# The last down-projection of a two-layer decoder as seven half-size products

## The chip, the cores and the metric

The kernel runs on one core of a Trainium2 chip. The metric is the device time of one execution in microseconds (us), the median over the runs shown; lower is better. The engines are TensorE (PE; the loads of its stationary operand are listed as PEld), VectorE (DVE), ScalarE (ACT), GpSimd (POOL) and SyncE (SP). SP, ACT and POOL each issue transfers on a queue of their own.

## The reference

A trunk of two layers works on `x` of 512 tokens by 1024 features: a Mamba-2 mixer and a gated FFN with a short convolution, then differential attention and a second such FFN. Only the end matters here:

```
def conv_ffn(x, ln_g, up_w, conv_w, conv_b, down_w):
    u = causal_dwconv(rms_norm(x, ln_g) @ up_w, conv_w, conv_b)
    gate, up = u[..., :FFN_DIM], u[..., FFN_DIM:]        # FFN_DIM = 2816
    return (jax.nn.silu(gate) * up) @ down_w             # (512 x 2816) @ (2816 x 1024)
...
    x = x + ff.astype(x.dtype)                           # the output of the last layer
```

All data is float32.

## The kernel before

Every large product is computed in a reduced format three times over: each operand is split into a high part (a copy rounded to `float32r` by ScalarE) and a low part (the difference, by VectorE), and `mm3` adds high x high, high x low and low x high into one PSUM bank (lines 170 to 172 of the kernel). The residual stream is kept feature-major: `xT[m]` holds features 128 m to 128 m + 127 of all 512 tokens.

**Weights.** A list `plan` names all weight chunks in the order of use. `emit_chunk` takes the next one: SP loads 512 KB into a `raw` tile (three buffers), ACT writes the high part `wh` (line 143), DVE the low part `wl` (line 144), three buffers each. `chunk(key)` hands a chunk to the matmuls and emits further ones, so that two are prepared ahead. The matmuls of a chunk of the FFN are 24, each 128x128 by 128x512.

**The FFN** (`ffn`). The 22 blocks of 128 hidden features are done in two passes, 12 and then 10. For each block, `u_block` computes the gate and then the up product (8 feature blocks, 24 matmuls each), scales by the norm (DVE, line 758), applies the convolution (one ACT operation, line 759, two DVE operations, line 761), and the block ends with SiLU (ACT), the product gate x up (DVE, line 774), and the split into `hh` (ACT, line 775) and `hl` (DVE, line 776). Then the down-projection of the pass follows: for each of four groups of 256 output features, three chunks of the weight feed two PSUM banks, with the weights stationary and the hidden activations of 512 tokens moving. DVE adds each bank to `xT[m]` (line 454).

**The end** (`store`). In the last pass of the last FFN, DVE adds each bank to the stream in two halves (line 800), PE transposes the sum to token-major (line 802), ACT copies it out of PSUM (line 803) and SP and ACT issue the transfers to `out` (line 804): 32 transposes in all.

**Order.** The program is written with tiles; a scheduler places the instructions on the engines by readiness and by their place in the program, adds all waits, and each engine then works strictly in the order so fixed. There are eight PSUM banks, four of tag `mm` and four of tag `aux`.

Of the kernel before, what the change touches and what calls it, by code (L numbers as in the profile page):

```python
# [9 lines left out]
F32 = mybir.dt.float32  # L10
F32R = mybir.dt.float32r
# [28 lines left out]
def trunk_kernel(ctx: ExitStack, tc, x, ssm_ln_g, ssm_in_w, ssm_conv_w, ssm_conv_b, ssm_dt_bias,  # L40
# [23 lines left out]
    def w_cols(w, k0, nk, c0, ncol):  # L64
        return w[k0 * P:(k0 + nk) * P, c0:c0 + ncol].rearrange("(k p) c -> p k c", p=P), nk, ncol
# [20 lines left out]
            out_chunks(g - 1)  # L86
    out_chunks(NG - 1)

    def ffn_plan(l):
        for h, (p0, p1) in enumerate(((0, HALF), (HALF, NPAIR))):  # L90
            for p in range(p0, p1):
                plan.append(("g%d_%d" % (l, p), *w_cols(ffn_up_w[l], 0, KB, p * P, P)))
                plan.append(("u%d_%d" % (l, p), *w_cols(ffn_up_w[l], 0, KB, FFN + p * P, P)))
# [20 lines left out]
    ffn_plan(1)  # L114

    AHEAD = 2
    ready = []
# [4 lines left out]
    def emit_chunk(pin=lambda i: i):  # L122
        i = state["next"]
        if i >= len(plan):
            return
        state["next"] = i + 1
        key, src = plan[i][:2]
        nk, ncol = plan[i][2:4]
# [4 lines left out]
        sync.dma_start(raw[:, :n].rearrange("p (k c) -> p k c", k=nk), src)  # L133
        if len(plan[i]) > 4:

            for k in range(nk):
                ks = slice(k * ncol, (k + 1) * ncol)
                g = c2[:, plan[i][4] + k:plan[i][4] + k + 1]
                act.activation(wh[:, ks], raw[:, ks], AF.Copy, scale=g)
                dve.scalar_tensor_tensor(out=wl[:, ks], in0=raw[:, ks], scalar=g,  # L140
                                         in1=wh[:, ks].bitcast(F32), op0=ALU.mult, op1=ALU.subtract)
        else:
            pin(act.activation(wh[:, :n], raw[:, :n], AF.Copy))  # L143
            pin(dve.tensor_tensor(out=wl[:, :n], in0=raw[:, :n], in1=wh[:, :n].bitcast(F32), op=ALU.subtract))  # L144
        ready.append((key, wh[:, :n].rearrange("p (k c) -> p k c", k=nk),
                      wl[:, :n].rearrange("p (k c) -> p k c", k=nk)))
# [39 lines left out]
    g1 = cp.tile([P, KB], F32, name="g1")  # L186
    rs = cp.tile([P, NT], F32, name="rs")

    xTt = rp.tile([P, KB, T], F32, name="xT")
    xT = [xTt[:, k, :] for k in range(KB)]  # L190
# [21 lines left out]
    with tc.tile_pool(name="ph0", bufs=1) as p0:  # L212
# [53 lines left out]
                                         op0=ALU.mult, op1=ALU.subtract))  # L266

        def keep(h, q, on):
            o = xTt[:, 2 * q:2 * q + 2, half[h]]
# [469 lines left out]
        run(out_proj(NG - 1, *prev, norm))  # L739


    def ffn(l, norm, bp, gnext, nnext):
        with tc.tile_pool(name="ffn_h%d" % l, bufs=1) as hp, tc.tile_pool(name="ffn%d" % l, bufs=1) as fp:
            rr = []

            def u_block(j, p):
                key = "%s%d_%d" % ("gu"[j], l, p)
                wh, wl = chunk(key)
                ps = mm_bank("ps_" + key)
                for k in range(KB):  # L750
                    mm3(ps, wh[:, k, :], wl[:, k, :], xgh[k], xgl[k], k == 0, k == KB - 1)
                if not rr:
                    rr.append(norm.row())
                r = rr[0]
                col = lambda t: cf[l][:, 88 * j + 22 * t + p:88 * j + 22 * t + p + 1]
                u = fp.tile([P, T], F32, tag="u", name="u" + key, bufs=3)
                v = fp.tile([P, T], F32, tag="v%d" % j, name="v" + key, bufs=3)
                dve.tensor_tensor(out=u, in0=ps, in1=r, op=ALU.mult)  # L758
# [4 lines left out]
                return v  # L763

            for p0, p1 in ((0, HALF), (HALF, NPAIR)):
                last = p1 == NPAIR
                hh, hl = [], []
# [12 lines left out]
                for c in range(4):  # L780
                    pss = [mm_bank("ps_d%d_%d_%d" % (l, p0, 2 * c + i)) for i in range(2)]
                    for k0 in range(0, n, 4):
                        wh, wl = chunk("d%d_%d_%d" % (l, c, p0 + k0))
                        for i in range(2):
                            for k in range(k0, min(n, k0 + 4)):
                                mm3(pss[i], wh[:, k - k0, i * P:(i + 1) * P],
                                    wl[:, k - k0, i * P:(i + 1) * P], hh[k], hl[k], k == 0, k == n - 1)
                    for i in range(2):
                        m = 2 * c + i
                        if last and nnext is None:  # L790
                            store(m, pss[i], fp)
                        else:
                            add_to_stream(m, pss[i], gnext, nnext if last else None)

    def store(m, ps, fp):
        pt = aux_bank("ot%d" % m)
        o = fp.tile([P, NT, P], F32, tag="o", name="o%d" % m, bufs=3)
        for j in range(2):
            h = slice(j * 256, (j + 1) * 256)
            dve.tensor_tensor(out=xT[m][:, h], in0=ps[:, h], in1=xT[m][:, h], op=ALU.add)  # L800
            for b in (2 * j, 2 * j + 1):
                pe.transpose(pt[:, b * P:(b + 1) * P], xT[m][:, b * P:(b + 1) * P], ident)
            act.activation(o[:, 2 * j:2 * j + 2, :], pt[:, h].rearrange("p (a b) -> p a b", a=2), AF.Copy)
            (sync if j else act).dma_start(
                out[0, h, m * P:(m + 1) * P].rearrange("(b p) c -> p b c", p=P), o[:, 2 * j:2 * j + 2, :])

    norm_kv = Norm(bp, "kv")
    ffn(0, norm, bp, None, norm_kv)
# [252 lines left out]
```

## Time and profile before

| what | value |
|---|---|
| median of 3 runs | 1394.48 us (1394.02 to 1394.83) |
| span of the profiled execution, first to last instruction | 1396.8 us (no other time of this execution is given) |
| PE busy | 1373.6 us, 98% |
| DVE busy | 916.4 us, 66% |
| ACT busy | 668.1 us, 48% |
| POOL busy | 94.2 us, 7% |
| mean granted TensorE clock | 0.991 of full speed |
| last FFN, from its first matmul to the end | 1023.3 to 1396.8 us |
| read from and written to DRAM | 131.72 MB, 2.25 MB |

Busy times are sums of instruction durations on one engine; matmuls overlap, so the time between the starts of two matmuls says more than the length of one. A row of the timeline gives the start in us, the duration in us, engine, line, operation, output and inputs, shapes and count, and in brackets the idle time before it with what ended it. A row of a group gives the busy time in us, the mean in ns, and the idle time ahead of the group's instructions by what ended it. "Landing" of a transfer is the time from its issue to its completion.

### The profile page before, as it was taken

Reading aid. Unit: us, or ns where it says so; the run is one execution under the profiler, and the core shown is the slowest. Engines: PE = TensorE matmul, PEld = TensorE weight load, DVE = VectorE, ACT = ScalarE, POOL = GpSimd, SP = SyncE. Lnnn points to the kernel's source line nnn. Section 1 sums busy time; section 2 is a strip of 40 time slices with the busy share of each in tenths; the row PEclk is TensorE's granted clock in tenths of the full one; section 3 lists DMA queues with packets and bytes.
Section 4 is the critical chain, followed back from the end, with each engine's and each line's share of the span. In section 5 each row is a group of like instructions: output and inputs, shape, how many; then the busy total and the mean of one; then the engine's idle time right before and its main releaser. Section 6 shows DMA issues by size and latency. Waiting matters only on the chain.

```text
span 1396.8 us, 17046 instructions
## 1 busy us (share of the span) xinstructions
PE 1373.6 (98%) x6475; PEld 1111.0 (80%) x6475; DVE 916.4 (66%) x1537; ACT 668.1 (48%) x1104; POOL 94.2 (7%) x120
## 2 busy tenths in 40 slices
PE   8999999999999999999999999999999999999998
PEld 6878787787788888888888787786778888888886
DVE  4889878678767775257754546747677774367741
ACT  4588553733254443134433547857654443144431
POOL 4140300300030000000001000000020000000000
PEclk8999999999999999999999999999999999999999
DMA  5463433422233332333323322221133333333332
GB/s 152 119 182 103 144 91 105 130 79 81 79 102 91 92 105 91 105 92 95 101 83 98 117 91 76 61 77 52 46 91 105 91 99 97 92 104 91 98 92 68
DMA packets 187620, 135.09 MB, mean 97 GB/s; under 512 B 6541, under 2 KB 176977, under 8 KB 187537
## 3 DMA queue, kind: packets, MB, share of 16 engines
q1 hardware_dynamic: 180736, 120.84, 29.3%
q0 software_dynamic: 4496, 12.05, 2.8%
q10 hardware_dynamic: 2304, 1.10, 0.3%
q8 instruction: 51, 0.84, 0.2%
q14 instruction: 33, 0.26, 0.1%
HBM read 131.72 MB, written 2.25 MB: 96 GB/s over the span
## 4 chain that ended last, share of the span: by engine, by line
PE 83%; DVE 7%; ACT 6%; issue 2%; DMA 1%; POOL 1%; POOLq 0%; SPq 0%; ACTq 0%; DVEq 0%
PE ps_u L170 6%; PE ps_u L171 6%; PE ps_u L172 6%; PE ps_d L170 6%; PE ps_d L171 6%; PE ps_d L172 6%; PE ps_g L170 6%; PE ps_g L171 6%; PE ps_g L172 6%; PE ps_in L172 4%; PE ps_in L171 4%; PE ps_in L170 4%; PE ps_o L171 2%; PE ps_o L172 2%; PE ps_o L170 2%
## 5 line engine op out<-in xcount | busy, mean ns | idle before, releaser
L170 PE MATMUL ps_u<-xgh,wh_u 128*128 128x512 f32 x352 | 137.9, 392 | 0.0
L171 PE MATMUL ps_u<-xgl,wh_u 128*128 128x512 f32 x352 | 137.7, 391 | 0.0
L171 PE MATMUL ps_g<-xgl,wh_g 128*128 128x512 f32 x352 | 137.0, 389 | 0.5 <-DVE xgl L366 0.5
L170 PE MATMUL ps_d<-hh,wh_d 128*128 128x512 f32 x352 | 137.5, 391 | 0.0
L172 PE MATMUL ps_u<-xgh,wl_u 128*128 128x512 f32 x352 | 137.4, 390 | 0.0
L172 PE MATMUL ps_d<-hh,wl_d 128*128 128x512 f32 x352 | 137.3, 390 | 0.0
L170 PE MATMUL ps_g<-xgh,wh_g 128*128 128x512 f32 x352 | 137.0, 389 | 0.0
L171 PE MATMUL ps_d<-hl,wh_d 128*128 128x512 f32 x352 | 137.0, 389 | 0.0
L172 PE MATMUL ps_g<-xgh,wl_g 128*128 128x512 f32 x352 | 136.9, 389 | 0.0
L171 PE MATMUL ps_in<-xgl,wh_in 128*128 128x512 f32 x312 | 123.6, 396 | 0.0
L170 PE MATMUL ps_in<-xgh,wh_in 128*128 128x512 f32 x312 | 123.3, 395 | 0.0
L172 PE MATMUL ps_in<-xgh,wl_in 128*128 128x512 f32 x312 | 122.6, 394 | 0.0
L144 DVE TENSOR_TENSOR wl_d<-wr_d,wh_d 128x1024 fp32r<-128x1024 f32 (+1 forms) x48 | 54.5, 1135 | 91.8 <-ACT wh_d L143 91.6
L143 ACT ACTIVATE wh_d<-wr_d 128x1024 fp32r<-128x1024 f32 (+1 forms) x48 | 47.5, 990 | 129.4 <-PE ps_d L171 115.3
L775 ACT ACTIVATE hh<-vg 128x512 fp32r<-128x512 f32 x44 | 27.8, 631 | 114.9 <-DVE vg L774 114.9
L758 DVE TENSOR_TENSOR uu<-ps_u,nr_f 128x512 f32<-128x512 f32 x44 | 30.4, 692 | 79.4 <-PE ps_u L172 79.4
L172 PEld LDWEIGHTS ps_u<-xgh,wl_u 128*128 128x128 f32 x352 | 66.5, 189 | 13.9
L171 PEld LDWEIGHTS ps_g<-xgl,wh_g 128*128 128x128 f32 x352 | 66.0, 188 | 14.4 <-DVE xgl L366 0.8
L170 PEld LDWEIGHTS ps_u<-xgh,wh_u 128*128 128x128 f32 x352 | 66.5, 189 | 13.8
L171 PEld LDWEIGHTS ps_u<-xgl,wh_u 128*128 128x128 f32 x352 | 66.5, 189 | 13.6
L170 PEld LDWEIGHTS ps_g<-xgh,wh_g 128*128 128x128 f32 x352 | 66.1, 188 | 14.1 <-ACT xgh L365 0.5
L172 PEld LDWEIGHTS ps_g<-xgh,wl_g 128*128 128x128 f32 x352 | 66.1, 188 | 13.8
(334 smaller groups left out, 3002.8 us busy)
## 6 DMA issues: line engine op xcount, KB each, us to landing
wr_g<-in_ffn_up_w_dram SPq DMA_DIRECT2D x44, 512.0 KB, 3.9
wr_u<-in_ffn_up_w_dram SPq DMA_DIRECT2D x44, 512.0 KB, 3.8
wr_in<-in_ssm_in_w_dram SPq DMA_DIRECT2D x40, 512.0 KB, 3.9
wr_d<-in_ffn_down_w_dram SPq DMA_DIRECT2D x40, 512.0 KB, 3.5
m<-cumd POOLq DMA_DIRECT2D x16, 512.0 KB, 4.2
wr_out<-in_ssm_out_w_dram SPq DMA_DIRECT2D x16, 512.0 KB, 3.5
wr_k<-in_kv_w_dram SPq DMA_DIRECT2D x8, 512.0 KB, 3.8
wr_q<-in_q_w_dram SPq DMA_DIRECT2D x8, 512.0 KB, 4.0
```

The source lines that it names most:

```text
L143: pin(act.activation(wh[:, :n], raw[:, :n], AF.Copy))
L144: pin(dve.tensor_tensor(out=wl[:, :n], in0=raw[:, :n], in1=wh[:, :n].bitcast(F32), op=ALU.subtract))
L170: pe.matmul(ps, wh, xh, start=start, stop=False)
L171: pe.matmul(ps, wh, xl, start=False, stop=False)
L172: pe.matmul(ps, wl, xh, start=False, stop=stop)
L758: dve.tensor_tensor(out=u, in0=ps, in1=r, op=ALU.mult)
L775: act.activation(h, ga, AF.Copy)
```

## The change

The last FFN gets a function of its own, `last_ffn`. Its down-projection uses Strassen's method (the variant with seven products and shared sums): tokens are split in two halves of 256, the K dimension in even and odd blocks of 128, and the output features in two halves of 512. Each of the seven products is a product of half the size in all three dimensions.

- **Residual.** `turn` transposes the stream into token-major tiles `xt[b]` (128 tokens by 1024 features) with 32 transposes and eight ACT copies, after the first two pairs of hidden blocks. The space of the feature-major stream is then used again for weights.
- **Hidden activations.** `hidden(q)` does the blocks 2q and 2q + 1, and DVE forms the four sums `S1` to `S4` (each 128x256); one ACT and one DVE instruction split all seven left operands (1792 columns) into `hh` and `hl`.
- **Weights.** `fetch` loads the four quadrants of the weight of a pass in 1 MB transfers on SP's queue, two pairs into the pass. `weights` forms the right operand of products 5, 6, 7 and 4 by a subtraction in place on DVE, and splits it (ACT, DVE), up to 1024 columns per chunk. The quadrants are no longer loaded through `raw`.
- **Passes.** There are three: pairs 0 to 3, 4 to 7, 8 to 10. In each, the chunks come in the order of `STEPS`: products 1, 5, 2 for the first two pairs, then for the others, then 6, 7, 3, 4. Hidden activations (128 tokens) are stationary and weights (512 columns) moving.
- **Results.** Product 1 starts bank X, and 6 and 7 go on adding to it; 5 starts Y, and 3 goes on; 2 and 4 have banks of their own. After each product `add` copies the bank with ACT into a tile `ev` (tag `u`, three buffers, shared with `u_block`) and GpSimd issues a transfer that adds it to its quadrant of `xt` (product 7 goes to two quadrants). In the last pass that holds for products 1, 5 and 6; the results of 2, 7, 3 and 4 are added by DVE from PSUM to `xt`, and SP and ACT send finished quadrants to `out` directly.

The core of the diff:

```
-    rp = ctx.enter_context(tc.tile_pool(name="residual", bufs=1, side="right"))
+    rp = ctx.enter_context(tc.tile_pool(name="residual", bufs=2, side="right"))
...
+    PASSES = ((0, 4), (4, 8), (8, 11))
+    STEPS = ((1, 5, 2), (6,), (7,), (3,), (4,))
...
-                v = fp.tile([P, T], F32, tag="v%d" % j, name="v" + key, bufs=3)
+                v = fp.tile([P, T], F32, tag="v%d" % j, name="v" + key, bufs=nb)      # 2 in last_ffn
...
+            def turn(b, c):
+                ps = aux_bank("xt%d_%d" % (b, c))
+                for k in range(4):
+                    pe.transpose(ps[:, k * P:(k + 1) * P], xT[4 * c + k][:, b * P:(b + 1) * P], ident)
+                act.activation(xt[b][:, c * 512:(c + 1) * 512], ps, AF.Copy)
+
+            def fetch(q0, q1):
+                raw = {}
+                for i in range(2):
+                    for j in range(2):
+                        n = q1 - q0
+                        t = (rp if i else hp).tile([P, 4, 512], F32, tag="x8", name="dr%d_%d%d" % (q0, i, j), bufs=2)
+                        rows = dw[2 * q0 * P:2 * q1 * P, j * 512:(j + 1) * 512]
+                        sync.dma_start(t[:, :n, :], rows.rearrange("(q i p) c -> i p q c", i=2, p=P)[i])
+                        raw[i, j] = t
+                fold["raw"] = raw
+
+            def weights(key, prod, q0, a, n):
...
+                if prod == 5:
+                    sub(b11, b12, b11)
+                elif prod == 6:
+                    sub(b11, b22, b11)
+                elif prod == 7:
+                    sub(b12, b22, b12)
+                elif prod == 4:
+                    sub(b21, b21, b11)
+                wh = wp.tile([P, 2, 512], F32R, tag="wh", name="wh_" + key)[:, :n, :]
+                wl = wp.tile([P, 2, 512], F32R, tag="wl", name="wl_" + key)[:, :n, :]
+                act.activation(wh, src, AF.Copy)
+                dve.tensor_tensor(out=wl, in0=src, in1=wh.bitcast(F32), op=ALU.subtract)
...
+            def hidden(q):
+                f = fp.tile([P, 8, 256], F32, tag="f", name="f%d" % q)
...
+                for o, x, y, op in ((S3, A11, A21, ALU.subtract), (S1, A21, A22, ALU.add),
+                                    (S2, S1, A11, ALU.subtract), (S4, A12, S2, ALU.subtract)):
+                    dve.tensor_tensor(out=f[:, o, :], in0=f[:, x, :], in1=f[:, y, :], op=op)
+                h = hp.tile([P, 7, 256], F32R, tag="hh", name="hh%d" % q, bufs=4)
+                w = hp.tile([P, 7, 256], F32R, tag="hl", name="hl%d" % q, bufs=4)
+                act.activation(fl(h), fl(f[:, :7, :]), AF.Copy)
+                dve.tensor_tensor(out=fl(w), in0=fl(f[:, :7, :]), in1=fl(h).bitcast(F32), op=ALU.subtract)
...
+                def add(ps, b, prod, tos):
+                    if not last or prod in (1, 5, 6):
+                        ev = fp.tile([P, 512], F32, tag="u", name="ev%d_%d%d" % (q0, prod, b), bufs=3)
+                        act.activation(ev, ps, AF.Copy)
+                        for to in tos:
+                            pool.dma_start(xt[2 * to[0] + b][:, to[1] * 512:(to[1] + 1) * 512], ev, accum_op=ALU.add)
+                        return
+                    for to in tos:
+                        tb = 2 * to[0] + b
+                        m = 2 if prod == 4 and b else 1
+                        n = 512 // m
+                        for i in range(m):
+                            cs = slice(to[1] * 512 + i * n, to[1] * 512 + (i + 1) * n)
+                            o = xt[tb][:, cs]
+                            dve.tensor_tensor(out=o, in0=ps[:, i * n:(i + 1) * n], in1=o, op=ALU.add)
+                            if whole[to] == prod:
+                                (act if i else sync).dma_start(out[0, tb * P:(tb + 1) * P, cs], o)
...
+                            for b in range(2):
+                                ts = slice(b * P, (b + 1) * P)
+                                for j in range(n):
+                                    q = a + j
+                                    hh, hl = [t[:, SIDE[prod], ts] for t in hs[q]]
+                                    kw = dict(skip_group_check=True)
+                                    pe.matmul(bank[b], hh, wh[:, j, :], start=start and q == 0, stop=False, **kw)
+                                    pe.matmul(bank[b], hl, wh[:, j, :], start=False, stop=False, **kw)
+                                    pe.matmul(bank[b], hh, wl[:, j, :], start=False, stop=q == q1 - q0 - 1, **kw)
+                                if (a, n) == cs[-1]:
+                                    add(bank[b], b, prod, tos)
...
+            for i, (q0, q1) in enumerate(PASSES):
+                hs = []
+                for q in range(q0, q1):
+                    if q == q0 + 2:
+                        fetch(q0, q1)
+                    hs.append(hidden(q))
+                    if i == 0 and q < 2:
+                        for b in range(2 * q, 2 * q + 2):
+                            turn(b, 0)
+                            turn(b, 1)
+                down(q0, q1, hs, i == len(PASSES) - 1)
...
-    ffn(1, norm1, bp, None, None)
+    last_ffn(1, norm1)
```

More of the change, by code (lines that the diff above doesn't have):

```diff
@@ L87, in trunk_kernel, with up_plan @@
     out_chunks(NG - 1)
+    def up_plan(l, p):
+        plan.append(("g%d_%d" % (l, p), *w_cols(ffn_up_w[l], 0, KB, p * P, P)))
+        plan.append(("u%d_%d" % (l, p), *w_cols(ffn_up_w[l], 0, KB, FFN + p * P, P)))
     def ffn_plan(l):
@@ L113, in trunk_kernel, with pair_chunks, fast_order @@
             plan.append(("ao%d_%d" % (i, c), *w_cols(attn_out_w[0], 4 * i, 4, c * 256, 256)))
-    ffn_plan(1)
+    PASSES = ((0, 4), (4, 8), (8, 11))
+    STEPS = ((1, 5, 2), (6,), (7,), (3,), (4,))
+    fold = {}
+    def pair_chunks(q0, q1):
+        return [(a, min(2, q1 - q0 - a)) for a in range(0, q1 - q0, 2)]
+    def fast_order(q0, q1):
+        for step in STEPS:
+            for a, n in pair_chunks(q0, q1):
+                for prod in step:
+                    yield prod, a, n
+    for q0, q1 in PASSES:
+        for p in range(2 * q0, 2 * q1):
+            up_plan(1, p)
+        for prod, a, n in fast_order(q0, q1):
+            plan.append(("f%d_%d_%d" % (prod, q0, a), (prod, q0, a, n)))
     AHEAD = 2
@@ L127, in emit_chunk @@
         key, src = plan[i][:2]
+        if len(plan[i]) == 2:
+            ready.append((key, *fold["weights"](key, *src)))
+            return
         nk, ncol = plan[i][2:4]
@@ L187, in trunk_kernel @@
     rs = cp.tile([P, NT], F32, name="rs")
-    xTt = rp.tile([P, KB, T], F32, name="xT")
-    xT = [xTt[:, k, :] for k in range(KB)]
+    xTt = [rp.tile([P, 4, T], F32, tag="x8", name="xT%d" % i) for i in range(2)]
+    xT = [xTt[k // 4][:, k % 4, :] for k in range(KB)]
     xgh = [gp.tile([P, T], F32R, name="xgh%d" % k) for k in range(KB)]
@@ L268, in keep @@
         def keep(h, q, on):
-            o = xTt[:, 2 * q:2 * q + 2, half[h]]
+            o = xTt[q // 2][:, 2 * (q % 2):2 * (q % 2) + 2, half[h]]
             pin(act.activation(o, pv[h][q], AF.Copy) if on is act else dve.tensor_copy(o, pv[h][q]))
@@ L739, in trunk_kernel, with u_blocks @@
         run(out_proj(NG - 1, *prev, norm))
[L742 to L743 removed]
+    def u_blocks(l, norm, fp, nb):
             rr = []
@@ L763, in u_block, with ffn @@
                 return v
+            return u_block
+    def ffn(l, norm, bp, gnext, nnext):
+        with tc.tile_pool(name="ffn_h%d" % l, bufs=1) as hp, tc.tile_pool(name="ffn%d" % l, bufs=1) as fp:
+            u_block = u_blocks(l, norm, fp, 3)
             for p0, p1 in ((0, HALF), (HALF, NPAIR)):
@@ L789, in ffn @@
                         m = 2 * c + i
[L790 to L805, printed above, removed]
+                        add_to_stream(m, pss[i], gnext, nnext if last else None)
```

39 lines of the change are left out of this document (37 added, 2 removed).

## The prediction

> **What bounds the kernel now.** I read the page's busy shares, then its chain that ended last, then busy time by stage of the last FFN.
>
> ```profile
> PE 1373.6 (98%) x6475; PEld 1111.0 (80%) x6475; DVE 916.4 (66%) x1537; ACT 668.1 (48%) x1104; POOL 94.2 (7%) x120
> PE 83%; DVE 7%; ACT 6%; issue 2%; DMA 1%; POOL 1%; POOLq 0%; SPq 0%; ACTq 0%; DVEq 0%
> 1035.00:1158.00 123.00, 123.00 (x546) 101.82 (x546) 89.38 (x114) 57.08 (x70) 0.00 (x0) 1.00 0.33 97
> 1158.00:1213.00 55.00, 55.00 (x245) 45.53 (x244) 19.90 (x21) 11.99 (x13) 0.00 (x0) 1.00 0.32 98
> 1213.00:1322.00 109.00, 109.00 (x482) 90.27 (x481) 72.02 (x90) 45.15 (x55) 0.00 (x0) 1.00 0.32 95
> 1322.00:1390.60 68.60, 68.60 (x313) 55.67 (x312) 26.18 (x39) 18.97 (x30) 0.00 (x0) 1.00 0.27 81
> 1390.60:1396.90 6.30, 1.52 (x9) 0.77 (x7) 0.76 (x2) 1.43 (x4) 0.00 (x0) 0.97 0.29 85
> ```
>
> The stage rows give length, then busy time of PE, PEld, DVE, ACT and POOL, clock, DMA share, GB/s. From 1035 us on PE never idles: the last FFN lasts as long as its matmuls, plus a tail of 6 us. DVE and ACT have much room in the two down stages (the rows at 1158 and 1322: DVE 36 to 38%), less in the up stages (73%).
>
> **Matmuls removed.** One weight chunk of the down-projection feeds 24 matmuls, and successive chunks come 5.44 us apart:
>
> ```profile
> 1197.74 1.23 DVE L144 TENSOR_TENSOR wl_d<-wr_d,wh_d 128x1024 fp32r<-128x1024 f32 x1 [4.21 <-ACT wh_d L143]
> 1203.18 1.23 DVE L144 TENSOR_TENSOR wl_d<-wr_d,wh_d 128x1024 fp32r<-128x1024 f32 x1 [4.21 <-ACT wh_d L143]
> ```
>
> That is 0.2267 us per 128x512 matmul. Before: 22 K blocks x 8 x 3 = 528. After: 7 products x 11 blocks x 2 token blocks x 3 = 462, same shape. 66 fewer: **-15.0 us**. Hidden activations are now stationary and weights moving; the K/Q/V projections already do that, with matmuls of the same length:
>
> ```profile
> L844 PE MATMUL ps_q<-wh_q,xgl x64: 387/389/482, 792.8 to 919.8; 128*128 128x512 f32 x64
> ```
>
> **Transposes.** The old store has 32, the new `turn` also 32, but eight of the old ones lie in the tail. Between the two starts below lie eight transposes and eight matmul intervals (1.81 us):
>
> ```profile
> 1346.05 0.39 PE L172 MATMUL ps_d<-hh,wl_d 128*128 128x512 f32 x1
> ...
> 1349.02 0.39 PE L171 MATMUL ps_d<-hl,wh_d 128*128 128x512 f32 x1
> ```
>
> 2.97 - 1.81 = 1.16 us for eight: **+1.2 us** net. Their eight ScalarE copies lie in the up stage, where ACT is 46% busy.
>
> **Tail.** Now: last matmul, DVE half, transposes, ACT, transfer.
>
> ```profile
> 1390.34 0.40 PE L172 MATMUL ps_d<-hh,wl_d 128*128 128x512 f32 x1
> 1390.77 0.76 DVE L800 TENSOR_TENSOR xT<-ps_d,xT 128x256 f32<-128x256 f32 x2 [0.61 <-PE ps_d L172]
> 1393.09 0.39 ACT L803 ACTIVATE o<-ot 128x256 f32<-128x256 f32 x1 [0.53 <-PE ot L802]
> out_dram<-o ACTq DMA_DIRECT2D x8, 128.0 KB, 3.7
> out_dram<-o SPq DMA_DIRECT2D x8, 128.0 KB, 2.5
> ```
>
> After, the transfer starts once the two DVE halves end (1391.53 on this clock) instead of 1393.48: 1.95 us earlier, but on ACT's queue, whose transfers land later. Between -1.95 and -0.75 I take **-1.8**, the last transfer having the engines to itself.
>
> **Start of a down pass.** Prices, and the chain behind the last up block:
>
> ```profile
> L143 ACT ACTIVATE wh_d<-wr_d 128x1024 fp32r<-128x1024 f32 x40 | 42.5, 1062 | 117.6 <-PE ps_d L171 105.3 <-PE ps_u L171 5.7 <-issue 5.5
> L143 ACT ACTIVATE wh_d<-wr_d 128x512 fp32r<-128x512 f32 x8 | 5.1, 633 | 11.8 <-PE ps_d L171 10.0 <-PE ps_u L171 1.9
> L144 DVE TENSOR_TENSOR wl_d<-wr_d,wh_d 128x1024 fp32r<-128x1024 f32 x40 | 49.0, 1226 | 91.8 <-ACT wh_d L143 91.6
> L144 DVE TENSOR_TENSOR wl_d<-wr_d,wh_d 128x512 fp32r<-128x512 f32 x8 | 5.5, 682 | 0.0
> L447 ACT ACTIVATE nr_f<-al_nf 128x512 f32<-128x512 f32 x2 | 1.2, 598 | 10.8 <-PE al_nf L408 10.8
> L800 DVE TENSOR_TENSOR xT<-ps_d,xT 128x256 f32<-128x256 f32 x16 | 5.9, 418 | 12.6 <-PE ps_d L172 12.6
> 1104.39 0.69 DVE L758 TENSOR_TENSOR uu<-ps_u,nr_f 128x512 f32<-128x512 f32 x1 [1.90 <-PE ps_u L172]
> 1109.36 0.69 DVE L776 TENSOR_TENSOR hl<-vg,hh 128x512 fp32r<-128x512 f32 x1 [0.70 <-ACT hh L775]
> ```
>
> The chain takes 5.66 us today. `hidden` lengthens it by three 256-wide sums (3 x 0.42) and by splitting 1792 columns instead of 512: from the two widths, 1.71 us on ACT (+1.07) and 2.04 on DVE (+1.35). Total 9.3 us, plus some 0.3 before it. The first step (products 1, 5, 2 on pairs 0 and 1) covers 36 matmuls, and the last pair's low half is read by the 40th: 9.07 us. So 0.5 us late, and up to 1.23 more if a weight split gets in front on DVE: 0.9 per pass, three passes, **+2.7** (0 to 5). In the up stages themselves the four sums and wider split add 2.3 us of DVE per 21.8 us: 73% becomes 83%, still covered. The fewer `v` buffers and the single `f` also cost nothing: what they hold is read within 10 us, and the next write to the same slot comes a pair (10.9 us) later.
>
> **Weights in the passes.** A chunk now serves 12 matmuls (2.72 us) for the same split, and products 5, 6, 7, 4 subtract first. Four-pair pass: PE 38 us; DVE 14 splits + 8 subtractions = 27 us plus 6.2 of the chain, of which 3.7 is done beforehand; ACT 14.9 of splits + 14 copies at 0.6 = 23. Covered, as three buffers give each chunk 5.44 us. The last pass (three pairs, PE 28.6 us) has splits 7 x 1.91, subtractions 4 x 1.91, chain 6.2, and seven products' results partly on DVE (adds at 0.69: 7.1): 34.3, less 3.7 done before and 0.8 after: 29.8 against 28.6. I take **+2.5** (0 to 6).
>
> **Accumulator banks.** Product 6 ends in bank X and product 7 goes on in it, so PE waits for ScalarE's copy (0.6 us, after up to 1.06 of a weight copy) with six matmuls, 1.36 us, of cover, three in the last pass: 0.5 per pass, **+1.5** (0 to 4).
>
> **Accumulating transfers.** None is in the trace; nearest are the other transfers on GpSimd's queue:
>
> ```profile
> DMA to landing us min/median/max: 1.8/4.0/10.2
> ```
>
> So the landing time L is 1.8 to 10.2 us; I take 4.0, the median over sizes 64 to 512 KB around this one's 256. The `ev` tiles share three buffers with `u`; copies of the first step want them 1.36 us apart. The fourth copy finds its buffer L - 3.4 us late, ACT's weight copies queue behind it, and the first copy of product 6, on which PE's bank waits, is late by 2 x (L - 4.85) in each of two passes. In the last pass DVE's add of product 2 waits for product 1's transfer, L - 4 more. At 4.0: **+1.0** for one late add; below nothing it can't be.
>
> **Fetch.** The quadrants come in 1 MB transfers on SP's queue, beside the up chunks:
>
> ```profile
> SPq L133 <- DVE wl_u L144: 89.9, 18, 5.0
> q1 hardware_dynamic: 180736, 120.84, 29.3%
> ```
>
> SP idles nearly a chunk before each load, waiting only for a raw buffer: three buffers and two prepared chunks put a load about 14 us ahead of its split (two chunks before use). 97 GB/s at a third of the engines means about 300 at most: 4 MB take some 14 us. Up chunks queued behind land just in time, with the 3 us that a split has to spare. I cost it at nothing; with that cover gone it is 3.9 us (a landing) per pass. The two transfers that reuse the residual's space also wait for `turn`, with 40 us to spare.
>
> **DVE beside GpSimd.** POOL's work doubled a DVE operation once, and didn't another time:
>
> ```profile
> 1024.91 1.36 POOL L442 TENSOR_TENSOR nacc_f<-nacc_f,nsq_f 128x512 f32<-128x512 f32 x1 [0.87 <-ACT nsq_f L441]
> 1025.04 1.77 DVE L366 SCALAR_TENSOR_TENSOR xgl<-xT,c,xgh 128x512 fp32r<-128x512 f32 x1
> 161.34 1.06 POOL L572 DMA_DIRECT2D er<-cumd  x2
> 161.95 0.69 DVE L641 TENSOR_TENSOR xs<-xs,er 128x512 f32<-128x512 f32 x1
> ```
>
> A GpSimd addition held DVE up by 1 us; GpSimd issuing transfers did not (0.69 us, as ever). The new 38 issues at 0.53 us are of the second kind: no cost. If they blocked like the addition, up to 20 us would be added to DVE. The Trainium skill (SBUF — State Buffer, Who interferes with whom) says that a two-input VectorE operation contends only with GpSimd instructions that read SBUF; by that rule, with which this trace agrees (0.69 us), the sum stays.
>
> **Clock.** Small PE gaps had one late effect:
>
> ```profile
> 1029.26 0.50 PE L171 MATMUL ps_g<-xgl,wh_g 128*128 128x512 f32 x1 [0.53 <-DVE xgl L366]
> 1031.89 0.63 PE L171 MATMUL ps_u<-xgl,wh_u 128*128 128x512 f32 x1
> 1032.32 0.63 PE L172 MATMUL ps_u<-xgh,wl_u 128*128 128x512 f32 x1
> ```
>
> After about 2.4 us of lost PE time, matmuls came 0.43 apart for some 3 us: 1.7 us more. My waits are under 1.5 us each, so I add nothing; by the row, three such episodes would give +5.1 and 1391.7. The Trainium skill (TensorE: Matmul & The Clock Gate, What's actually happening) halves the clock only after a window of 3.4 us idle; by that rule the sum stays, though this trace already shows less idling followed by slow matmuls.
>
> **Sum.** -15.0 - 1.8 + 1.2 + 2.7 + 2.5 + 1.5 + 1.0 = -7.9 us. The profiled span of 1396.8 would become 1388.9; it is 2.3 us above the runs' median 1394.48, so the median becomes **1386.6**.
>
> **Rivals.**
> - *All waits covered*: only -15.0 - 1.8 + 1.2 remain: 1378.9. For it: DVE and ACT idle over half of the old down stages, and subtractions depend only on older ones, so can be placed early. Against: the pass start is late by count. Chance 0.14.
> - *DVE becomes the bound*: subtract, copy, split in strict order take 1.23 + 1.06 + 1.23 + 0.15 = 3.67 us for 2.72 of PE. Over the four chunks of products 6 and 7 that is 3.8 less 1.8 of slack, 2 us in each of three passes, and 6 instead of 2.5 in the last: +9.5, so 1396. For it: the 29.8 against 28.6. Chance 0.17.
> - *Accumulating transfers too slow* (the other side): the loss 4 x (L - 4.85) + (L - 4), less the 1.0 counted already, eats the 7.9 at L = 6.5 us. At 8 us it is 15.6: 1402. For it: 10.2 as the queue's maximum, and an addition must fetch its destination too. Against: the median of 4.0. Chance 0.22.
>
> **How the numbers follow.** The forecast, with its own range 1382 to 1391.5, has the remaining 0.47. A measurement of this kernel tells about 0.2% (2.8 us) from no change. Faster: 0.47 + 0.14 = 0.61; within: 0.17; slower: 0.22. The range reaches from the covered case to the slow transfers at 8 us: 1378 to 1403. What it leaves out is the far end of the slow transfers.
>
> **What would show it.** After: 462 matmuls at 0.227 us in the down passes; PE idle summed over the last FFN near 8 us, in three spots (first read of the last pair, product 7's first matmul, last pass); the chain ending DVE to ACT's queue, under 5 us after the last matmul; accumulating transfers landing near 4 us. PE waits on ScalarE's copies with GpSimd transfers behind them would mean the third rival; on `wl` in products 6 and 7, the second. The prediction is wrong if transfers of the quadrants hold up the up chunks.

## The result: slower, where faster was forecast

| kernel | median | runs |
|---|---|---|
| before | 1394.65 us | 1394.02 to 1399.16 |
| after | 1405.62 us | 1400.93 to 1406.93 |

The ratio over the runs is 1.0063, 95% interval 1.0048 to 1.0079: slower by 8.8 us (the two medians lie 11.0 us apart), where 7.9 us less was forecast.

The page of after, the rows that answer to those of before:

```profile
PE 1363.4 (97%) x6409; PEld 1097.2 (78%) x6409; DVE 978.8 (70%) x1599; ACT 702.9 (50%) x1137; POOL 127.5 (9%) x158
...
q0 software_dynamic: 9968, 22.02, 6.7%
```

PE is busy for 10 us less, yet the span is 1399.2 us. The part that the change touches is the last FFN, from its first gate matmul to the end: 373.5 us before (1023.3 to 1396.8), 382.5 after (1016.7 to 1399.2). The instructions ahead of it stand in the same order in both kernels; their length differs between executions (a second profile of after has the first gate matmul at 1020.8, and 381.7 us for the last FFN). The last FFN is thus 9.0 us longer, as much as the ratio gives for the whole kernel, and the comparisons below go by its length and by the ratios.

Busy time by stage of the last FFN after (down pass 1, the up stage behind it, down pass 2, a full up stage left out, down pass 3; columns as in the stage table of before):

```profile
1112.06:1161.42 49.36, 42.55 (x169) 33.05 (x168) 27.89 (x28) 23.21 (x28) 12.17 (x14) 0.93 0.60 135
1161.42:1248.46 87.04, 87.04 (x385) 72.07 (x384) 69.60 (x88) 38.29 (x45) 1.72 (x2) 1.00 0.43 117
1248.46:1295.83 47.37, 41.34 (x170) 32.22 (x168) 28.32 (x28) 23.39 (x29) 12.12 (x14) 0.93 0.59 127
...
1361.11:1394.55 33.44, 30.41 (x127) 22.99 (x125) 25.16 (x35) 14.90 (x20) 5.21 (x6) 1.00 0.41 95
```

PE is busy all through the two later up stages (87.04 of 87.04 us, and 65.28 of 65.28 us in the one left out): neither the fetch nor the longer chain costs anything there. The 168 matmuls of a four-pair pass need 38.1 us at 0.2267 each, and the passes take 49.4 and 47.4; the last needs 28.6 and takes 33.4. That is 11.3 + 9.3 + 4.9 = 25.5 us lost, and the clock is below 1.00 in two passes. What PE waited for in the last FFN (us in total, times, longest):

```profile
PE ps_x L928 <- ACT ev L901: 11.0, 2, 5.9
PE ps_x L928 <- ACT hh L885: 2.2, 1, 2.2
PE ps_x L929 <- DVE hl L886: 2.1, 3, 0.8
```

The first row is the signature that the prediction gave for its third rival: product 7 waits for ScalarE's copy of product 6's bank. The chain behind it in the first pass, from the timelines of ACT, GpSimd, SP and PE:

```profile
1127.99 1.09 ACT L901 ACTIVATE ev<-ps_x 128x512 f32<-128x512 f32 x2 [3.29 <-PE ps_x L930]
1129.91 0.60 ACT L901 ACTIVATE ev<-ps_y 128x512 f32<-128x512 f32 x1
1132.35 0.60 ACT L901 ACTIVATE ev<-ps_y 128x512 f32<-128x512 f32 x1 [0.90 <-DMA xt<-ev]
1141.42 0.60 ACT L901 ACTIVATE ev<-ps_x 128x512 f32<-128x512 f32 x1 [4.25 <-DMA xt<-ev]
1128.89 2.76 POOL L903 DMA_DIRECT2D xt<-ev  x3 [105.14 <-ACT ev L901]
1133.24 0.85 POOL L903 DMA_DIRECT2D xt<-ev  x1 [1.59 <-ACT ev L901]
1132.74 23.21 SPq L844 DMA_DIRECT2D dr<-in_ffn_down_w_dram  x4
1135.77 0.39 PE L930 MATMUL ps_x<-wl_f,hh 128*128 128x512 f32 x1
1142.07 0.79 PE L928 MATMUL ps_x<-wh_f,hh 128*128 128x512 f32 x1 [5.91 <-ACT ev L901]
1142.66 0.63 PE L929 MATMUL ps_x<-wh_f,hl 128*128 128x512 f32 x1
```

Three copies fill the three buffers at once, as both halves of product 1 end together. The fourth waits for the first transfer (issued 1128.89, buffer free 1132.35: 3.46 us). The seventh, the first of product 6, waits for the fourth transfer: issued 1133.24, free 1141.42, so 8.2 us. PE could have gone on at 1136.0, does at 1142.07, and then runs at 0.43 us per matmul. The transfers' landing (us; first all 38, then those of the first down pass with the loads beside them, then those of the last pass):

```profile
DMA to landing us min/median/max: 3.3/7.0/9.8
xt<-ev POOLq DMA_DIRECT2D x16, 256.0 KB, 7.4
dr<-in_ffn_down_w_dram SPq DMA_DIRECT2D x4, 1024.0 KB, 7.3
xt<-ev POOLq DMA_DIRECT2D x6, 256.0 KB, 4.5
```

In the first two passes the four 1 MB loads for the next pass go out beside them (from 1132.74 on in the first): 7.4 us. The program has these loads in the middle of the next up stage; the scheduler issues them as soon as their space is free, a stage earlier. In the last pass, with no fetch, 4.5 us, and no wait on `ev`.

### The profile page after: what moved, and what is told of

It is laid out like the page before. It is cut to its first block, busy times and chain, and to the rows that moved or that the text cites. A ratio compares the mean times of both kernels' runs of the same rounds, so it can differ in the third digit from the quotient of the medians.

```text
span 1399.2 us, 17097 instructions
## 1 busy us (share of the span) xinstructions
PE 1363.4 (97%) x6409; PEld 1097.2 (78%) x6409; DVE 978.8 (70%) x1599; ACT 702.9 (50%) x1137; POOL 127.5 (9%) x158
## 4 chain that ended last, share of the span: by engine, by line
PE 81%; DVE 8%; ACT 6%; issue 3%; DMA 1%; POOL 1%; SPq 0%; DVEq 0%; ACTq 0%; POOLq 0%
PE ps_u L194 6%; PE ps_u L195 6%; PE ps_u L196 6%; PE ps_g L195 6%; PE ps_g L194 6%; PE ps_g L196 6%; PE ps_in L196 4%; PE ps_in L195 4%; PE ps_in L194 4%; PE ps_d L195 3%; PE ps_d L196 3%; PE ps_d L194 3%; PE ps_o L195 2%; PE ps_o L196 2%; PE ps_o L194 2%
## 5 line engine op out<-in xcount | busy, mean ns | idle before, releaser
L167 ACT ACTIVATE wh_u<-wr_u 128x1024 fp32r<-128x1024 f32 x44 | 46.8, 1063 | 69.1 <-PE ps_g L195 58.2
L195 PEld LDWEIGHTS ps_u<-xgl,wh_u 128*128 128x128 f32 x352 | 66.5, 189 | 13.8
L194 PEld LDWEIGHTS ps_u<-xgh,wh_u 128*128 128x128 f32 x352 | 66.4, 189 | 13.8
L864 DVE TENSOR_TENSOR wl_f<-dr,wh_f 128x1024 fp32r<-128x1024 f32 (+1 forms) x42 | 47.2, 1132 | 37.9 <-ACT wh_f L863 36.3
L194 PE MATMUL ps_d<-hh,wh_d 128*128 128x512 f32 x176 | 68.5, 389 | 0.0
L195 PE MATMUL ps_d<-hl,wh_d 128*128 128x512 f32 x176 | 68.5, 389 | 0.0
L196 PE MATMUL ps_d<-hh,wl_d 128*128 128x512 f32 x176 | 68.5, 389 | 0.0
L196 PEld LDWEIGHTS ps_in<-xgh,wl_in 128*128 128x128 f32 x312 | 58.6, 188 | 12.5 <-issue 1.1
```

The source lines that it names most:

```text
L194: pe.matmul(ps, wh, xh, start=start, stop=False)
L195: pe.matmul(ps, wh, xl, start=False, stop=False)
L196: pe.matmul(ps, wl, xh, start=False, stop=stop)
L864: dve.tensor_tensor(out=wl, in0=src, in1=wh.bitcast(F32), op=ALU.subtract)
```

## The experiments

The theory: three things meet, a bunch of results, three buffers, and a landing that the fetch stretches. Main rival: the 16 DMA engines are simply full, so more buffers would only move the wait. The kernel before ran beside each set (medians 1396.29, 1395.94 and 1396.67 us), and every ratio is to it. An interval reaches some 0.0015, or 2 us, to each side. The last column comes from one execution each and has a difference that isn't of the edits: behind the same short waits at its start, the first up stage has a stretch of matmuls at half clock in most of these executions (granted clock 0.87 and 0.79 in two stretches of 5 us of after), but none in those of e1, e3, e5 and e8 (1.00), where this stage is 1.5 us shorter (93.9 to 94.0 us, against 95.4 in after).

| run | edit | ratio | 95% interval | last FFN, us |
|---|---|---|---|---|
| e1 | six buffers | 0.9964 | 0.9948 to 0.9979 | 367.4 |
| e2 | late fetch | 0.9986 | 0.9973 to 0.9999 | 371.1 |
| e3 | plain copy | 0.9988 | 0.9975 to 1.0002 | 371.8 |
| e4 | VectorE adds | 0.9958 | 0.9944 to 0.9972 | 367.8 |
| e5 | split in parts | 0.9914 | 0.9898 to 0.9929 | 360.2 |
| e6 | e1 and e5 | 0.9950 | 0.9931 to 0.9968 | 365.0 |
| e7 | e1 and e2 | 0.9941 | 0.9924 to 0.9957 | 367.6 |
| e8 | e4 and e5 | 0.9942 | 0.9922 to 0.9963 | 363.6 |
| e9 | e1, e2 and e5 | 0.9905 | 0.9888 to 0.9923 | 359.8 |
| e10 | e2 and e5 | 0.9898 | 0.9883 to 0.9913 | 359.9 |
| e11 | matmuls in the wait | 1.0034 | 1.0017 to 1.0052 | 378.6 |
| after, again | none | 1.0062 | 1.0047 to 1.0077 | 381.7 |

**e1, six buffers.**

```
-ev = fp.tile([P, 512], F32, tag="u", ..., bufs=3)
+hold, tag, nb = ((fp, "u", 3), (bp, "nsq", 2), (fp, "u", 3), (bp, "nacc", 1), (fp, "u", 3), (bp, "nsq", 2))[evs[0] % 6]
+evs[0] += 1
+ev = hold.tile([P, 512], F32, tag=tag, ..., bufs=nb)
```

> Edit: the evicted results of the down passes rotate over six buffers instead of the three shared with the up stage's u; nothing else. Theory 1 (buffers): three buffers with a landing of about 7 us hold up ScalarE's copies, PE waits for them on product 6's banks (11.0 us in two waits) and then runs two windows of 3.4 us at half clock per run; with six buffers both waits go, PE's idle time on ev falls from 11.0 us to under 1, no granted clock of 0.5 remains in the down passes, and the time falls by some 14 to 17 us, to 1385 to 1391. Theory 2 (rate): accumulating transfers and the fetch of the next quadrants share 16 DMA engines that are 9/10 busy, so six buffers only stretch the landing (from 7 us to over 10) and the wait comes back at a later product: under 5 us gained, over 1400.

What PE waited for in e1, and the landings in its first down pass and behind it:

```profile
PE ps_x L931 <- ACT hh L886: 2.5, 1, 2.5
PE ps_x L932 <- DVE hl L887: 2.0, 3, 0.8
...
xt<-ev POOLq DMA_DIRECT2D x16, 256.0 KB, 10.0
wr_u<-in_ffn_up_w_dram SPq DMA_DIRECT2D x2, 512.0 KB, 18.9
```

The wait on `ev` is gone, and 1.0063 - 0.9964, or 13.8 us, with it (by the trace 15.1, of which 1.5 are the shorter first up stage). So buffers were what turned the landing into a loss. Half clock was expected to be gone from the down passes and isn't: in the last the granted clock is 0.58 behind the wait on `hh` of 2.5 us (1364.8 to 1367.6). The rival has a share: the landing grew to 10.0 us, and a load for the up stage behind the fetch took 18.9 us and cost PE 0.5 us twice. The contention moved, but to where it was nearly covered.

**e2, late fetch.** Pins the quadrants' loads, and those of all gate and up chunks of the last FFN, to their place in the program.

```
+if key[:3] in ("g1_", "u1_"):
+    tc.keep_in_program_order(ld)
...
-sync.dma_start(t[:, :n, :], rows...)
+pin(sync.dma_start(t[:, :n, :], rows...))
```

> Edit: on SP's queue the four 1 MB loads of the next pass's quadrants keep their place in the program, in the middle of the up stage, and no longer go out while the down pass before them still accumulates. Theory 1 (three buffers with a landing time L): in passes 0 and 1 L falls from about 7 us to the 4.5 us that the last pass shows without a fetch, and the two PE waits on ev shrink to under 1 us each; 10 to 17 us less. Theory 2 (the accumulating transfers are slow by themselves): L stays near 7 and the waits stay; no change. Cost expected beside it: the quadrants meet the up chunks, 0 to 4 us per pass.

What PE waited for, and the landing in the first pass:

```profile
PE ps_x L930 <- ACT ev L903: 2.8, 2, 1.4
xt<-ev POOLq DMA_DIRECT2D x16, 256.0 KB, 4.3
```

The landing fell to 4.3 us, with additions, buffers and split as they were: the fetch is what stretched it. 10.7 us came back by the ratios, and the waits shrank to 1.4 us each, not below one. The transfers alone are thus too slow for three buffers and bunched results, though the prediction's condition (L below 4.85) was met; with six buffers as well (e7) no wait on `ev` is left.

**e3, plain copy.** The addition of six of the seven products is left out.

```
-pool.dma_start(xt[...][...], ev, accum_op=ALU.add)
+pool.dma_start(xt[...][...], ev)
```

> Edit: the same transfers of the same size to the same places, but they overwrite the residual and do not add to it (the addition of six of the seven products is left out). If the addition is what makes the transfers slow, L falls from 7.0 us to 4 or less, the PE waits on ev go and the time falls by 14 to 17 us. If contention with the fetch is enough to make them slow, L stays at 6 or more and the waits stay within 2 us of theirs.

PE's wait, the landings of the first and last pass, and the queue's share of the DMA engines:

```profile
PE ps_x L928 <- ACT ev L901: 4.3, 2, 2.4
xt<-ev POOLq DMA_DIRECT2D x16, 256.0 KB, 5.6
xt<-ev POOLq DMA_DIRECT2D x6, 256.0 KB, 2.3
q0 software_dynamic: 7536, 22.02, 4.7%
```

Neither expectation: with the fetch beside it 5.6 us instead of 7.4, without it 2.3 instead of 4.5. The addition adds about 2 us to the landing, the fetch about 3. Of the queue's share, 2.7% is there without these transfers (e4). What is left is 4.0% of 1399.2 us for 38 transfers with addition, 1.47 us of all sixteen engines each, against 2.0% of 1392.8, 0.73 us, for plain ones: adding doubles the engine time.

**e4, VectorE adds all results.**

```
-if not last or prod in (1, 5, 6):
+if False:
```

> Edit: no accumulating transfers; VectorE adds every product's result from PSUM to the residual, 16 additions of 0.69 us in each of the first two passes. All waits on ev must be gone. If the rival of the prediction by which VectorE becomes the bound holds, its 11 us per pass cost most of what the waits gave back: PE waits on wl in products 6 and 7, time 1393 to 1400. If VectorE's slack covers them (36% busy in the down stages before the change), the time is as with six buffers, 1385 to 1391.

PE's waits in e4, and the queue's share:

```profile
PE ps_y L928 <- ACT wh_f L863: 2.8, 3, 0.9
q0 software_dynamic: 4496, 12.05, 2.7%
```

The second case: as fast as six buffers. VectorE's 11 us per pass are covered but for three waits of 0.9 us, 2.8 us in all, on a high half from ScalarE at product 3 and not on `wl` in products 6 and 7; the prediction's second rival (VectorE as the bound) had 9.5. The edit does one thing more: the branch that is now always taken also sends a quadrant to `out`, so 18 transfers of unfinished quadrants, 14 of them of 256 KB, go out in the first two passes and are overwritten later. The result is right, but the times of e4 and e8 contain these transfers.

**e5, split in parts.** S3 and A11 are split after a pair's first up block, then A12, A22 and S1, then S2 and S4.

```
-A12, A22, S1, S2, S3, S4, A11, A21 = range(8)
+A12, A22, S1, S2, S4, S3, A11, A21 = range(8)
...
-act.activation(fl(h), fl(f[:, :7, :]), AF.Copy)
-dve.tensor_tensor(out=fl(w), in0=fl(f[:, :7, :]), in1=fl(h).bitcast(F32), op=ALU.subtract)
+    if i == 0:
+        sums((S3, A11, A21, ALU.subtract)); split(S3, A11 + 1)
+sums((S1, A21, A22, ALU.add)); split(A12, S1 + 1)
+sums((S2, S1, A11, ALU.subtract), (S4, A12, S2, ALU.subtract)); split(S2, S4 + 1)
```

> Edit: a pair's left operands are split in three parts as they become ready (the difference S3 and A11 after the first up block, then A12, A22, S1, then S2, S4) in place of one split of seven after the second; buffers and transfers are those of the change. The prediction put the late start of the three passes at 2.7 us; the trace after shows 6.7 us above the pure matmul time (1.7, 1.7, 3.3). If the one long split is the cause, the PE waits on hh and hl (2.2 and 2.1 us) go and the excess falls to under 2 us; the waits on ev stay near 11 us, so the time falls by 3 to 6 us, to 1399 to 1403. If the low halves of the weights are what is late there, nothing changes.

Measured: 20.8 us less than the change, where 3 to 6 were expected; the wait on `ev` was expected to stay and is gone. The largest PE wait left in the down passes, the landing, the first, fourth and seventh of ScalarE's copies (the seventh is the first of product 6), the fourth transfer, the fetch, and the start of product 7:

```profile
PE ps_y L942 <- DVE wl_f L864: 1.1, 1, 1.1
xt<-ev POOLq DMA_DIRECT2D x16, 256.0 KB, 7.3
1125.10 0.58 ACT L913 ACTIVATE ev<-ps_x 128x512 f32<-128x512 f32 x1
1129.43 0.60 ACT L913 ACTIVATE ev<-ps_y 128x512 f32<-128x512 f32 x1 [1.32 <-DMA xt<-ev]
1135.23 0.60 ACT L913 ACTIVATE ev<-ps_x 128x512 f32<-128x512 f32 x1
1130.32 0.85 POOL L915 DMA_DIRECT2D xt<-ev  x1 [1.06 <-ACT ev L913]
1133.89 13.50 SPq L844 DMA_DIRECT2D dr<-in_ffn_down_w_dram  x4
1136.34 0.39 PE L940 MATMUL ps_x<-wh_f,hh 128*128 128x512 f32 x1
```

The median landing is as bad as ever (7.3 us), but not where it mattered. The first copy comes at 1125.10, and PE goes on with product 7 at 1136.34 without a wait, 11.2 us later; in the changed kernel product 1's last matmuls had to wait for the late operands, its first copy came at 1127.99, and PE could have gone on at 1136.0, 8.0 us later. And the fourth transfer is issued 3.6 us ahead of the fetch (1130.32 against 1133.89), no longer 0.5 us behind it. So the late pass start and the waits on the transfers were not two losses to be added: the stall bunched the six results. By the rows, spacing and fetch have about equal parts: from the fourth transfer's issue to product 7 there are 6.0 us instead of 2.8, and the buffer is free after at most 4.9 us (the copy at 1135.23 waits for no transfer) instead of 8.2.

One loss is left in e5. The first step of the second pass takes 3.1 us more than its 72 matmuls (0.4 in the first pass), more than the 1.7 of the changed kernel, so the expected excess of under 2 us wasn't reached. PE's waits there lead to VectorE. In e10, which differs by the late fetch alone, it is 0.4.

**e6, six buffers and parts.** The two edits above together.

> Edit: six buffers and the split in parts together. The two waits lie in different places (pass start; product 6's banks), so their gains should add: six buffers alone were 0.9964 of the time before, the parts should take another 4 to 5 us: ratio 0.992 to 0.994, 1385 to 1388. If they don't add, the pass start was cover for ScalarE's copies and the wait on ev comes back.

It missed: slower than parts alone. A row of ACT's timeline in the up stage behind the first pass, and busy time there, of e6 and (second) of e5:

```profile
1169.57 1.06 ACT L167 ACTIVATE wh_u<-wr_u 128x1024 fp32r<-128x1024 f32 x1 [10.82 <-DMA wr_u<-in_ffn_up_w_dram]
1160.00:1180.00 20.00, 20.00 (x90) 16.57 (x89) 8.08 (x11) 5.12 (x7) 0.86 (x1) 1.00 0.83 209
```

```profile
1160.00:1180.00 20.00, 20.00 (x90) 16.55 (x89) 13.09 (x17) 8.74 (x11) 0.86 (x1) 1.00 0.67 175
```

An up load arrives late, ACT sits for 10.8 us on it, and VectorE does 8.1 us of work in that stretch instead of 13.1. PE doesn't stop, but VectorE, over 80% busy for the rest of the stage, doesn't make it up: the next pass starts with PE waiting 1.9 us for VectorE. The first step of that pass takes 4.7 us more than its matmuls, where e5 had 3.1. Of the 4.8 us between e6 and e5 by the trace, 1.5 are the first up stage and 3.3 lie in the second and third pass; that the late load makes all of the 3.3 isn't shown. Here the main rival came true: the faster the copies leave, the harder they press on the loads.

**e7, six buffers and late fetch; e10, parts and late fetch.**

> Edit: six buffers and late fetch, the left operands still split at once at the end. Neither buffers nor fetch can hold product 6's copies up, so only the late pass start is left of the loss: 6.7 us by the trace after. With all three edits the time was 0.9905 of the time before; this one should be 5 to 7 us above, ratio 0.994 to 0.996. If it is at 0.9905 too, the pass start costs nothing by itself and mattered only through the copies that it bunched.

> Edit: split in parts and late fetch, the three buffers of the change kept. With parts the first step's six results end about 1.4 us apart and not within 2.6 us, so with landings of 4.3 us three buffers suffice (the sum's condition L < 4.85): no PE wait on ev, ratio 0.989 to 0.991, as with all three edits, 1380 to 1383. If three buffers are too few by themselves, PE waits on ev in product 7 return and it is above 0.993.

PE's two longest waits in the last FFN in e7, and the longest in e10, which lies in an up stage:

```profile
PE ps_x L933 <- ACT hh L888: 2.2, 1, 2.2
PE ps_x L934 <- DVE hl L889: 2.1, 3, 0.8
```

```profile
PE ps_g L197 <- DVE xgl L392: 0.5, 1, 0.5
...
```

Both as expected. What stands between them, 0.9941 - 0.9898 or 6.0 us, is the price of the late pass start by itself; they differ in the buffers too, but e7 and e9, which differ by the split alone, lie 5.0 us apart by the ratios and 7.8 by the trace. In e10 no wait in a down pass is left, three buffers suffice, and it is the fastest kernel here with e9: 1381.89 us, 1.0% faster than the kernel before and 1.6% faster than the change. Against e5 the late fetch brings 2.2 us, and the intervals of the two overlap. It has a price: a chunk of the first up stage reaches PE 0.5 us late in every run with the late fetch.

**e9, all three edits.**

> Edit: six buffers, split in parts, and the fetch of the quadrants at its program place. With six buffers the accumulating transfers landed in 10.0 us beside the fetch and held up one up chunk (0.5 and 0.5 us of PE in the up stage). Late fetch should bring landings back to 4.3 us and free that chunk: 1 us or less beside six buffers with parts, ratio 0.991 to 0.994. If the quadrants, now in the middle of the up stage, hold up other up chunks, it is slower than without by up to 3 us.

0.9905: just below the expected range, and within the interval of e10, so six buffers add nothing measurable once the others are done. Against e6, the late fetch alone is worth 6 us; 1 us or less was expected, as e6's own loss wasn't known.

**e8, VectorE adds and parts.**

> Edit: additions by VectorE from PSUM, no accumulating transfers, and the split in parts. VectorE's three 0.9 us waits at product 3 (its weights' high halves come late) stay. Expected 0.9958 less 4 to 5 us: ratio 0.992 to 0.993. If VectorE is near its bound, the earlier parts of the split push the weights' low halves back, and the gain is under 2 us.

0.9942 against 0.9958 without parts, or 2.2 us, with overlapping intervals; by the trace 4.2 us, of which 1.5 are the shorter first up stage. The three waits of 0.9 us stay. ACT's wait for VectorE's subtractions grew:

```profile
ACT wh_f L863 <- DVE dr L851: 29.1, 6, 5.9
```

In e4, as in the changed kernel, this row was 11.2 us, in e5 15.6. VectorE has less room once it does everything; that it is at its bound isn't shown, and the gain lies between the two expectations.

**e11, matmuls in the wait.** 36 matmuls more, with a result that isn't used.

```
+if prod == 7 and a == 0 and not last:
+    for r in range(18):
+        pin(pe.matmul(W[0], hs[0][0][:, SIDE[7], :P], hs[0][0][:, 0:2, :]..., start=True, stop=True))
```

> Edit: the changed kernel with 18 added matmuls (4.1 us) ahead of product 7 in each of the first two passes; they write product 4's bank, which product 4 later starts afresh, so they add nothing to the result. They lie inside the PE waits of 5.9 and 5.1 us on ScalarE's copies, so PE idles only 1 to 2 us there. If the windows of half clock (matmuls 0.43 us apart for some 3.4 us after each wait) come from the idling itself, they disappear, the wait on the copies stays where it ends, and the time falls by 4 to 6 us although more is computed. If half clock comes from something else (the transfers beside it), it stays and the time doesn't change.

> The changed kernel unaltered, on the same chip as the others of this set: ratio 1.005 to 1.008 by the first result. It is the point from which e11, six buffers with late fetch, and parts with late fetch are measured.

The stretches behind product 7's first matmul in the first two passes, of e11 and (second) of after, the third column from the right being the granted clock:

```profile
1142.60:1146.00 3.40, 3.31 (x14) 2.62 (x15) 1.22 (x1) 1.89 (x4) 1.71 (x2) 1.00 1.06 336
1276.20:1279.60 3.40, 3.32 (x14) 2.63 (x15) 1.23 (x1) 1.88 (x4) 1.72 (x2) 1.00 0.94 275
```

```profile
1143.00:1146.50 3.50, 3.50 (x9) 2.63 (x8) 1.22 (x1) 0.48 (x1) 1.02 (x2) 0.50 1.09 329
1278.00:1281.50 3.50, 3.50 (x9) 2.72 (x9) 1.23 (x1) 1.08 (x2) 1.66 (x2) 0.52 1.10 313
```

With the DMA engines about as busy as before (1.06 against 1.09, 0.94 against 1.10) the half clock is gone, and 1.0062 - 1.0034, or 3.9 us, with it, just under what was expected. That fits its length: in after, matmuls come 0.43 us apart from 1142.07 to 1148.2 and from 1277.70 to 1281.3, not for 3.4 us each but for 9.7 us in all, of which 0.2267 / 0.43 would have been enough, so 4.6 us are lost. PE still waits 1.5 and 1.8 us in e11, without half clock behind it. The half clock came from PE's idling; a kernel that computes 36 matmuls more is faster.

## Why the prediction was wrong

Its third rival came true, with the place and the signature that it named (chance 0.22). By its own terms, in us of the last FFN:

| term | predicted | measured |
|---|---|---|
| matmuls | -15.0 | -15.0: 44 from 1112.06 to 1122.04 us, 0.227 each; a pass of 168 without waits takes 38.6 us (e10), 0.5 more than that |
| transposes | +1.2 | -0.1: 2 x 1.67 for the 32, where 24 had cost 3 x 1.16 |
| tail | -1.8 | -1.4: 5.05 us from the start of the last matmul, before 6.46 |
| start of a down pass | +2.7 | +6.7: 1.7, 1.7 and 3.3 |
| last pass, VectorE | +2.5 | +1.4, what that pass loses beyond its late start |
| accumulator banks and accumulating transfers | +2.5 | +17.2: 11.0 of waits, some 4.6 of half clock, the rest small gaps |
| fetch | 0 | no PE wait of its own; it stretched the landing from 4.3 (e2) to 7.4 |
| clock | 0 | 3.9 of the 17.2 by e11 |
| sum | -7.9 | +8.8 (the trace: +9.0) |

**The step that failed is the term of the accumulating transfers**, and in three places. *The landing*: 4.0 us was taken, the median of transfers that don't add; 7.0 was measured. Against a plain transfer alone (2.3), the addition brings about 2 us (e3) and the fetch about 3 (e2). The prediction had bounded the landing by 1.8 and 10.2, and 7.0 lies inside; it was wrong to sit near the middle when its text names one reason that points up (an addition must fetch its destination) and the fetch was a second. By its own formula 4.0 us would cost nothing, so its +1.0 was a guess. *The condition*: 4.85 us was counted for results 1.36 us apart, as if the pass ran without a stall, while two terms higher up the same sum has the pass stall. With results in a bunch, e2's 4.3 us still cost 1.4 us per pass. With L = 7.0 the prediction's own formula gives 1397; the other 6 (by the ratio) to 8 us are the bunching, the clock and the pass start. *The sum itself*: it added terms that feed each other. e5, meant to remove at most 6 us, removed 20.8.

**Start of a down pass**: the mechanism was right, the size wrong. VectorE between the last up product and the low half in the first pass:

```profile
1112.26 0.69 DVE L781 TENSOR_TENSOR uu<-ps_u,nr_f 128x512 f32<-128x512 f32 x1
1113.13 1.23 DVE L864 TENSOR_TENSOR wl_f<-dr,wh_f 128x1024 fp32r<-128x1024 f32 x1 [0.17 <-ACT wh_f L863]
...
1119.60 0.42 DVE L882 TENSOR_TENSOR f<-f 128x256 f32<-128x256 f32 x1
1119.93 1.22 DVE L851 TENSOR_TENSOR dr<-dr,dr 128x1024 f32<-128x1024 f32 x1
...
1125.15 2.02 DVE L886 TENSOR_TENSOR hl<-f,hh 128x1792 fp32r<-128x1792 f32 x1
```

From 1112.26 to 1127.17 VectorE hardly pauses, and between the steps of the chain stand eight splits and subtractions of weights of 1.22 us each. The prediction added the chain's own steps to 9.6 us and allowed for one such operation; it is 14.9. In the four-pair passes the third pair's 18 matmuls cover some of that, which the prediction hadn't counted; in the last pass they aren't there, and it waits longest.

**Fetch**: costed at nothing because PE wouldn't wait for the loads, and PE didn't; ScalarE waited 3.4 us for one up load behind the first pass. The prediction placed the fetch beside the up chunks, where the program has it; for the second and third pass it went out in the down pass before, in the middle of the additions. And it asked whether the fetch would be late, not whom it would make late: the transfers on the other queue.

**Clock**: the prediction said that three small episodes might cost 5.1 us but that its waits were under 1.5 us. Given waits of 5 us, the half clock follows. The rule that it weighed (the Trainium skill, TensorE: Matmul & The Clock Gate, What's actually happening: half clock after an idle window of 3.4 us) agrees with the waits of 5.1 and 5.9 us; in e3 an idle time of 2.4 us was followed by matmuls 0.43 us apart as well, and one of 2.0 wasn't; the same wait of 2.2 us in the last pass was in e3 and wasn't in the changed kernel.

**Right**: VectorE beside GpSimd's issues. While GpSimd issued three transfers (1128.89 to 1131.65) a split took what it always takes:

```profile
1130.05 1.22 DVE L864 TENSOR_TENSOR wl_f<-dr,wh_f 128x1024 fp32r<-128x1024 f32 x1 [1.75 <-ACT wh_f L863]
```

So was the tail's chain, the longer chain in the up stages at no cost, and that VectorE's total wouldn't be the bound.

## What to carry to other kernels

Waits that a sum lists as separate terms may feed each other: a stall ahead of a burst of results shortens the time in which a ring of buffers has to come free, so work out each term with the others' delays put in. When a transfer is moved to a time where another queue is at work, ask not only whether it is in time but what it makes late; and price an unknown kind of transfer from the side to which the reasons point. A change that loses may be one dependency away from a gain: here the last FFN was 13.6 us shorter than before (373.5 to 359.9) once operands came in parts and the fetch left the transfers alone, and most of that came with the parts.

## What the runs showed of the hardware

- A transfer that adds to SBUF takes twice the DMA engine time of a plain one of the same size (1.47 against 0.73 us of all sixteen engines for 256 KB), and GpSimd 0.86 us to issue it, against 0.54 for a plain one. Alone it lands in 4.5 us, a plain one in 2.3.
- An idle time of PE costs more than itself: waits of 5.9 and 5.1 us were followed by 6.1 and 3.6 us at half clock, and filling them with unused matmuls made the kernel 3.9 us faster. The border isn't sharp: idle times of 2.0 to 2.6 us had the effect in some places and not in others, the same wait of 2.2 us in e3 and not in the changed kernel.
- A load that arrives late needn't stop PE to cost time: in e6 VectorE lost 5 us of work some 80 us before PE waited for it.
